# A two-layer hybrid decoder on one core: the whole program in one block, ordered against the library's timeline simulation

## The chip, the core and the metric

The kernel runs on one core of one Trainium2 chip. The metric is device time in microseconds (us) of one execution. Three executions of the kernel before took 1261.02, 1261.59 and 1265.77 us; the median is 1261.59 us.

## The reference

The input x is 512 tokens by 1024 channels, float32. Each of two layers does the following, all in float32:

```
h    = rmsnorm(x, attn_norm_w)
proj = h @ w_in                                  # z, xbc, dt, sc_*, q, k/v of three branches, gates
y_ssd = ssd_mixer(...)       # conv of width 4 + silu, chunked state-space scan (8 heads of 64, state 128), gated norm
y_sc  = sc_b * causal_dwconv(sc_c * sc_h)        # short convolution
y_nsa = nsa_mixer(...)       # 4 heads of 64: compressed, selected and window attention, weighted by gates
x = x + concat(y_ssd, y_sc, y_nsa) @ w_out
h = rmsnorm(x, ffn_norm_w)
gate, val = split(causal_dwconv(h @ w_up) + b)   # width 3, 2 x 2752 channels
x = x + (silu(gate) * val) @ w_down
```

and a last norm follows.

## The kernel before

Activations lie transposed, channels on the 128 partitions and the 512 tokens along a row. Every large product is made of three matmuls per 128x128 weight block (`mul3`, L188 to L190): weights and activations are each split into a rounded part and the rest (the weights by ACT L165 and then DVE or POOL L166), and the three significant cross products are accumulated in PSUM. One output tile of the input projection is 8 blocks, so 24 matmuls. In what follows these matmuls are called filler, since they can be placed wherever the rest leaves room.

A layer has three stretches. The first is the start: the norm's sums (ACT L224 squares, DVE L228 and L234 add, PE L236), their reciprocal root spread back over the partitions (DVE L201, POOL L202, PE L205, ACT L244), a group of narrow products (L450, L451) and the first projection tiles; rope (DVE L266 to L268), a split of keys (L282, L308) and the key compression (PE L468) follow. The second is attention: 32 head scores (PE L597 and L600, DVE L602 adds the mask and takes the row extreme, ACT L604 is the exponential, DVE L606 to L608 and DVE or POOL L610 scale it), each transposed by PE (L618), split by ACT L622 and DVE L625, and multiplied with the values (PE L637, tile `pv`, of which there is one). Between these pieces stand the projection's filler, the evacuation of its tiles (DVE L359) with the width-4 convolution (DVE L363, L365), and the small chain on time steps (`ssd_dt`, DVE L662 to L677). The third is the scan (L704 to L822) with its own norm, then the output projection. The gated MLP comes last, 65 tiles of up and down products, pure filler with its own evacuations.

The program is written in an order in which the pieces of attention and scan alternate with pieces of the projection, by weights in a table (`PLAN`). That text isn't yet the order on the engines. The library's tile layer takes the instructions as written and orders each engine's queue with a list scheduler that asks a simulation which instruction is ready and when; some instructions are kept in the order of the text (`pinned`). Each engine then runs its own queue strictly in order, and waits on semaphores where an operand comes from another engine. Line 1157 opens this scope:

```
with _tile.TileContext(nc) as tc:
    trunk(tc, ins, out)
```

Of the kernel before, what the change touches and what calls it, by code (L numbers as in the profile page):

```python
# [63 lines left out]
def trunk(ctx: ExitStack, tc: tile.TileContext, ins, out):  # L64
    nc = tc.nc
    V, A, G, TE = nc.vector, nc.scalar, nc.gpsimd, nc.tensor

    per = ctx.enter_context(tc.tile_pool(name="per", bufs=1))
    pw = ctx.enter_context(tc.tile_pool(name="pw", bufs=3))
    ph = ctx.enter_context(tc.tile_pool(name="ph", bufs=1))  # L70
# [1091 lines left out]
```

## Time and profile before

| | before |
|---|---|
| median of three executions | 1261.59 us |
| profiled execution | 1265.31 us, its span 1263.5 us |
| PE busy | 1208.4 us, 96% |
| DVE busy | 879.8 us, 70% |
| ACT, POOL busy | 580.8 and 221.8 us |
| mean granted clock of PE | 0.981 |

The profiled execution is 3.7 us, 0.3%, above the median, and 1.8 us of it lie outside its span. The span has five parts by time: mixers of layer 0 (0 to 253 us), MLP of layer 0 (253 to 632), mixers of layer 1 (632 to 885), MLP of layer 1 (885 to 1233), and the last norm with the output (1233 to 1263.5). A share of busy time over the whole span hides these parts, so the rows below take each by itself.

### The profile page before, as it was taken

Reading aid. Unit: us, or ns where it says so; the run is one execution under the profiler, and the core shown is the slowest. Engines: PE = TensorE matmul, PEld = TensorE weight load, DVE = VectorE, ACT = ScalarE, POOL = GpSimd, SP = SyncE. Lnnn points to the kernel's source line nnn. Section 1 sums busy time; section 2 is a strip of 40 time slices with the busy share of each in tenths; the row PEclk is TensorE's granted clock in tenths of the full one; section 3 lists DMA queues with packets and bytes.
Section 4 is the critical chain, followed back from the end, with each engine's and each line's share of the span. In section 5 each row is a group of like instructions: output and inputs, shape, how many; then the busy total and the mean of one; then the engine's idle time right before and its main releaser. Section 6 shows DMA issues by size and latency. Waiting matters only on the chain. (4 is left out here: it accounts for less than half of the span.)

```text
span 1263.5 us, 15487 instructions
## 1 busy us (share of the span) xinstructions
PE 1208.4 (96%) x5843; PEld 999.2 (79%) x5843; DVE 879.8 (70%) x1408; ACT 580.8 (46%) x909; POOL 221.8 (18%) x199
## 2 busy tenths in 40 slices
PE   8889899999999999999999888999999999999997
PEld 7667678788888888888877666778888888888897
DVE  6899979567776247776468998794587743677763
ACT  6655554354443124444347455434444422444553
POOL 3442337500000000000043332563000000000001
PEclk9989999999999999999999899999999999999999
DMA  7321123233223332332223211322233323333352
GB/s 259 113 67 51 51 84 101 67 100 98 88 98 100 100 99 90 95 117 87 84 84 100 67 51 51 103 98 83 84 100 101 100 88 96 100 100 100 122 165 99
DMA packets 37051, 121.33 MB, mean 96 GB/s; under 512 B 4144, under 2 KB 6512, under 8 KB 36976
## 3 DMA queue, kind: packets, MB, share of 16 engines
q1 hardware_dynamic: 36832, 120.33, 30.0%
q8 instruction: 46, 0.75, 0.3%
q14 instruction: 29, 0.24, 0.1%
q10 hardware_dynamic: 144, 0.00, 0.0%
HBM read 118.19 MB, written 2.13 MB: 95 GB/s over the span
## 5 line engine op out<-in xcount | busy, mean ns | idle before, releaser
L188 PE MATMUL mm<-h,hl 128*128 128x512 f32 x1040 | 413.6, 398 | 0.8 <-DVE s L359 0.8
L189 PE MATMUL mm<-h,hl 128*128 128x512 f32 x1040 | 410.3, 395 | 0.0
L190 PE MATMUL mm<-h,hl 128*128 128x512 f32 x1040 | 409.7, 394 | 0.0
L165 ACT ACTIVATE hl<-raw 128x1024 fp32r<-128x1024 f32 (+1 forms) x211 | 220.8, 1047 | 236.9 <-PE mm L190 129.5
L166 DVE TENSOR_TENSOR hl<-raw,hl 128x1024 fp32r<-128x1024 f32 (+1 forms) x167 | 203.4, 1219 | 110.3 <-ACT hl L165 108.1
L188 PEld LDWEIGHTS mm<-h,hl 128*128 128x128 f32 x1040 | 197.8, 190 | 42.0 <-issue 1.8
L190 PEld LDWEIGHTS mm<-h,hl 128*128 128x128 f32 x1040 | 197.4, 190 | 41.2 <-issue 0.2
L189 PEld LDWEIGHTS mm<-h,hl 128*128 128x128 f32 x1040 | 197.7, 190 | 39.6 <-issue 0.5
L202 POOL TENSOR_TENSOR m<-m,mhalf 128x1 f32<-128x1 f32 (+2 forms) x14 | 9.9, 709 | 773.7 <-DVE m L201 773.7
L166 POOL TENSOR_TENSOR hl<-raw,hl 128x1024 fp32r<-128x1024 f32 x44 | 108.3, 2464 | 150.5 <-ACT hl L165 144.8
L928 DVE SCALAR_TENSOR_TENSOR s<-s,par 128x511 f32<-128x511 f32 (+1 forms) x172 | 128.3, 748 | 3.5 <-ACT s L926 0.6
L925 DVE TENSOR_TENSOR s<-mm,rstdB 128x512 f32<-128x512 f32 x86 | 59.1, 689 | 66.1 <-PE mm L190 66.1
L189 PE MATMUL mm<-s,hl 128*128 128x512 f32 (+1 forms) x240 | 86.6, 361 | 3.4 <-DVE s L248 3.4
L188 PE MATMUL mm<-s,hl 128*128 128x512 f32 (+1 forms) x240 | 86.5, 360 | 1.1 <-ACT s L247 1.1
L190 PE MATMUL mm<-s,hl 128*128 128x512 f32 (+1 forms) x240 | 86.4, 360 | 0.0
L247 ACT ACTIVATE s<-s 128x512 fp32r<-128x512 f32 (+1 forms) x62 | 33.0, 545 | 111.8 <-DVE s L943 108.0
L188 PE MATMUL aux<-s,hl 128*128 128x512 f32 (+1 forms) x232 | 82.1, 354 | 0.0
L190 PE MATMUL aux<-s,hl 128*128 128x512 f32 (+1 forms) x232 | 81.8, 353 | 0.0
L189 PE MATMUL aux<-s,hl 128*128 128x512 f32 (+1 forms) x232 | 81.8, 353 | 0.0
L926 ACT ACTIVATE s<-s,par 128x512 f32<-128x512 f32 x86 | 69.2, 807 | 8.8 <-DVE s L925 8.1
L248 DVE TENSOR_TENSOR s<-s 128x512 fp32r<-128x512 f32 (+1 forms) x62 | 45.3, 741 | 27.9 <-ACT s L247 27.9
L941 ACT ACTIVATE s<-s 128x512 f32<-128x512 f32 x40 | 25.3, 632 | 79.0 <-DVE s L928 79.0
(252 smaller groups left out, 1648.9 us busy)
## 6 DMA issues: line engine op xcount, KB each, us to landing
raw<-in_w_up SPq DMA_DIRECT2D x86, 512.0 KB, 3.5
raw<-in_w_dn SPq DMA_DIRECT2D x54, 512.0 KB, 3.5
raw<-in_w_in SPq DMA_DIRECT2D x44, 512.0 KB, 3.5
raw<-in_w_out SPq DMA_DIRECT2D x16, 512.0 KB, 3.6
raw<-in_w SPq DMA_DIRECT2D x8, 512.0 KB, 3.6
s<-dr SPq DMA_DIRECT2D x16, 256.0 KB, 4.3
x<-in_xT SPq DMA_DIRECT2D x8, 256.0 KB, 5.8
out<-s SPq DMA_DIRECT2D x8, 256.0 KB, 3.4
```

What stands on the lines that cost most here:

```text
L165: A.activation(t[:, 0, a:b], r[:, a:b], AF.Copy)
L166: eng.tensor_tensor(t[:, 1, a:b], r[:, a:b], t[:, 0, a:b].bitcast(F32), op=OP.subtract)
L188: TE.matmul(ps, wh, rhs_h, start=first, stop=False)
L189: TE.matmul(ps, wh, rhs_l, start=False, stop=False)
L190: TE.matmul(ps, wl, rhs_h, start=False, stop=last)
L202: G.tensor_tensor(dst, v, mhalf[:, :n], op=OP.pow)
L247: A.activation(dst_h, src, AF.Copy)
L248: V.tensor_tensor(dst_l, src, dst_h.bitcast(F32), op=OP.subtract)
L925: V.tensor_tensor(u, ps, rstdB, op=OP.mult)
L926: A.activation(acc, u, AF.Identity, scale=w[:, 2:3], bias=pr[:, C_FCB + i:C_FCB + i + 1])
L928: V.scalar_tensor_tensor(acc[:, j:], u[:, :T - j], w[:, 2 - j:3 - j], acc[:, j:], op0=OP.mult, op1=OP.add)
L941: A.activation(g, g, AF.Silu)
```

## The change

```
@@ -65,6 +65,7 @@
     nc = tc.nc
     V, A, G, TE = nc.vector, nc.scalar, nc.gpsimd, nc.tensor
 
+    ctx.enter_context(tc.block(schedule_with_timeline_sim=True))
     per = ctx.enter_context(tc.tile_pool(name="per", bufs=1))
     pw = ctx.enter_context(tc.tile_pool(name="pw", bufs=3))
     ph = ctx.enter_context(tc.tile_pool(name="ph", bufs=1))
```

The whole program now stands in one block, and the order of each queue in that block is made with another simulation of the library, which keeps a timeline of the engines. No instruction is added to the work and none leaves it; each stays on its engine, and tiles and buffers are the same. Every line after L67 has a number higher by one. What differs is the order within the queues, nearly all of it in the two mixers. Three places follow, before and now.

The first is ACT at the start of layer 0, from the group's bias (L335, now L336) on. `rstdB` is the norm's factor spread over the partitions, on which the rope tables on DVE wait. Before:

```order
L335 ACTIVATE btmp<-aux,m 128x148 x2
L259 ACTIVATE s<-mm 128x512
L165 ACTIVATE hl<-raw 128x1024
L261 ACTIVATE s<-s 32x512
L262 ACTIVATE s<-s 32x512
L335 ACTIVATE btmp<-aux,m 128x148 x2
L347 ACTIVATE s<-s 128x4x64 x2
L350 ACTIVATE gate<-bS 128x48
L244 ACTIVATE rstdB<-pv 128x512
```

Now:

```order
L336 ACTIVATE btmp<-aux,m 128x148 x2
L166 ACTIVATE hl<-raw 128x1024 x2
L260 ACTIVATE s<-mm 128x512
L245 ACTIVATE rstdB<-pv 128x512
L262 ACTIVATE s<-s 32x512
L263 ACTIVATE s<-s 32x512
L166 ACTIVATE hl<-raw 128x1024
L336 ACTIVATE btmp<-aux,m 128x148 x2
```

The factor has moved ahead of the two copies of rope and of the second pair of bias rows. On DVE the product Cr (L399, now L400) has moved with it, ahead of the second pair of L336. On PE the spread (L205) stands 101 matmuls into the program, and stood 119 into it; the key compression (L468) stands at 197 and stood at 188.

The second is PE in the middle of layer 0's attention, where its scores of 256 columns (`128x256`) begin. `mm<-h` is filler. Before:

```order
L637 MATMUL pv<-s 128x512 x2
L618 MATMUL aux<-cst,s 128x128 x4
L190 MATMUL mm<-h_81,hl 128x512
L188 MATMUL mm<-h_82,hl 128x512
L637 MATMUL pv<-s 128x512
L189 MATMUL mm<-h_82,hl 128x512
L190 MATMUL mm<-h_82,hl 128x512
L188 MATMUL mm<-h_83,hl 128x512
L637 MATMUL pv<-s 128x512
L597 MATMUL aux<-s 128x256
```

Now:

```order
L638 MATMUL pv<-s 128x512 x2
L619 MATMUL aux<-cst,s 128x128 x4
L638 MATMUL pv<-s 128x512 x2
L598 MATMUL aux<-s 128x256
L601 MATMUL aux<-s 128x256
L598 MATMUL aux<-s 128x256
L601 MATMUL aux<-s 128x256
L598 MATMUL aux<-s 128x256
L601 MATMUL aux<-s 128x256
L189 MATMUL mm<-h_80,hl 128x512
```

The filler between the pieces of attention is gone; the last row here is the first of 23 filler matmuls in one lump. In matmuls 230 to 800 of the program there are now 29 runs of filler and 11 of them have 17 matmuls or more, where 48 runs stood before with 3 such; in layer 1 it is 27 with 10, where it was 48 with 3.

The third is DVE at the head of attention. `m` of `128x32` is the chain on time steps, `s<-aux,s` (L625, now L626) is the rest of a transposed score, without which the value product on PE can't be finished. Before:

```order
L666 RECIPROCAL m<-m 128x32
L625 TENSOR_TENSOR s<-aux,s 128x512
L667 TENSOR_TENSOR m<-m 128x32
L359 TENSOR_TENSOR s<-mm,rstdB 128x512
L668 TENSOR_TENSOR m<-m 128x32
L669 TENSOR_SCALAR m<-m 128x32
L671 SCALAR_TENSOR_TENSOR m<-m 128x32 x3
L363 SCALAR_TENSOR_TENSOR s<-s,cwh 128x511
L671 SCALAR_TENSOR_TENSOR m<-m 128x32
L625 TENSOR_TENSOR s<-aux,s 128x512
```

Now:

```order
L667 RECIPROCAL m<-m 128x32
L609 TENSOR_TENSOR m<-m,gate 128x4
L668 TENSOR_TENSOR m<-m 128x32
L611 TENSOR_SCALAR s<-s,m 128x512 x2
L669 TENSOR_TENSOR m<-m 128x32
L670 TENSOR_SCALAR m<-m 128x32
L672 SCALAR_TENSOR_TENSOR m<-m 128x32 x6
L673 SCALAR_TENSOR_TENSOR m<-m 128x32
L675 SCALAR_TENSOR_TENSOR dtk<-m 128x32
L678 SCALAR_TENSOR_TENSOR aa<-dtk,m 128x32
L626 TENSOR_TENSOR s<-aux,s 128x512
L360 TENSOR_TENSOR s<-mm,rstdB 128x512
```

The first of the rests has moved behind the whole chain, and the evacuation of a projection tile (L359, now L360) with it.

Elsewhere: in the scan two chunks now interleave where one followed the other; five matmuls of the output projection are written ahead of the scan's last products; in the MLP of either layer the spread of its norm stands 13 matmuls later, with 11 filler matmuls instead of 24 between it and the first matmul of the third tile; in layer 1's start the spread stands 14 matmuls later, L468 13 later, and ACT does two weight copies and one evacuation ahead of two copies of rope.

## Rows read from the trace of the kernel before

**Rows 1.** From the page: engines' busy us (share); a group's busy us, mean ns.

```profile
PE 1208.4 (96%) x5843; PEld 999.2 (79%) x5843; DVE 879.8 (70%) x1408; ACT 580.8 (46%) x909; POOL 221.8 (18%) x199
...
L165 ACT ACTIVATE hl<-raw 128x1024 fp32r<-128x1024 f32 (+1 forms) x211 | 220.8, 1047 | 236.9 <-PE mm L190 129.5
```

**Rows 2.** Five stretches: stretch, length, busy us (instructions) by engine, clock, DMA share, GB/s.

```profile
0.00:253.00 253.00, 228.37 (x1119) 182.88 (x1120) 205.54 (x404) 135.15 (x259) 110.17 (x98) 0.95 0.30 99
253.00:632.00 379.00, 378.86 (x1681) 313.47 (x1680) 237.54 (x298) 155.03 (x194) 1.41 (x2) 1.00 0.31 96
632.00:885.00 253.00, 231.44 (x1162) 186.17 (x1162) 200.80 (x401) 132.08 (x253) 103.56 (x91) 0.97 0.25 80
885.00:1233.00 348.00, 347.95 (x1708) 295.33 (x1707) 224.64 (x288) 148.99 (x189) 3.86 (x5) 1.00 0.34 106
1233.00:1263.50 30.50, 21.73 (x180) 21.32 (x178) 11.23 (x22) 9.58 (x18) 2.79 (x4) 0.90 0.28 94
```

**Rows 3.** The same view, attention and scan of either layer.

```profile
60.00:160.00 100.00, 88.44 (x417) 69.29 (x417) 92.67 (x196) 53.68 (x118) 35.06 (x24) 0.93 0.20 63
160.00:253.00 93.00, 88.61 (x468) 71.36 (x467) 68.80 (x150) 39.94 (x77) 50.81 (x51) 0.98 0.27 86
690.00:790.00 100.00, 86.28 (x423) 67.22 (x422) 90.19 (x190) 52.75 (x117) 32.63 (x25) 0.95 0.18 54
790.00:885.00 95.00, 90.84 (x471) 73.91 (x470) 69.76 (x137) 40.91 (x68) 49.29 (x46) 0.98 0.29 95
```

**Rows 4.** Waits of PE, 0 to 260 us: total, times, longest.

```profile
PE pv L637 <- DVE s L625: 6.3, 6, 2.1
PE aux L468 <- DVE s L308: 4.2, 1, 4.2
...
PE mm L189 <- DVE s L248: 1.7, 1, 1.7
```

**Rows 5.** The same wait in layer 1, 620 to 860 us.

```profile
PE aux L468 <- DVE s L308: 3.1, 1, 3.1
```

**Rows 6.** Waits of DVE, 20 to 60 us.

```profile
DVE s L336 <- ACT btmp L335: 4.5, 2, 3.0
```

**Rows 7.** Timeline of PE: start, us, instruction, idle before and its releaser.

```profile
48.29 3.00 PE L468 MATMUL aux<-hl,s 128*64 128x256 f32 x16 [4.17 <-DVE s L308]
51.09 0.63 PE L190 MATMUL mm<-h,hl 128*128 128x512 f32 x1
51.52 0.63 PE L188 MATMUL mm<-h,hl 128*128 128x512 f32 x1
...
59.06 0.50 PE L597 MATMUL aux<-s 128*128 128x512 f32 x1 [1.22 <-DVE s L325]
```

**Rows 8.** Timeline of ACT at the first norm.

```profile
30.87 0.58 ACT L244 ACTIVATE rstdB<-pv 128x512 f32<-128x512 f32 x1
```

**Rows 9.** Timeline of DVE at the first norm.

```profile
31.48 0.69 DVE L399 TENSOR_TENSOR Cr<-rot,rstdB 128x512 f32<-128x512 f32 x1
...
47.07 1.17 DVE L308 TENSOR_TENSOR s<-s 128x256 fp32r<-128x256 f32 x2
```

**Rows 10.** Timeline of DVE, 76 to 86 us.

```profile
76.59 0.63 DVE L625 TENSOR_TENSOR s<-aux,s 128x512 fp32r<-128x512 f32 x1
...
82.94 2.34 DVE L671 SCALAR_TENSOR_TENSOR m<-m 128x32 f32<-128x32 f32 x1
...
85.80 0.17 DVE L671 SCALAR_TENSOR_TENSOR m<-m 128x32 f32<-128x32 f32 x1
```

**Rows 11.** Timeline of PE at the second value product.

```profile
85.94 0.50 PE L637 MATMUL pv<-s 128*128 128x512 f32 x1 [1.57 <-DVE s L625]
...
87.22 0.63 PE L190 MATMUL mm<-h,hl 128*128 128x512 f32 x1
```

**Rows 12.** Timeline at the start of layer 0's gated MLP, PE and DVE.

```profile
288.64 0.60 PE L205 MATMUL pv<-cst,m 128*128 128x128 f32 x4
...
291.12 1.28 DVE L925 TENSOR_TENSOR s<-mm,rstdB 128x512 f32<-128x512 f32 x2
```

More of the change, by code (lines that the diff above doesn't have):

```diff
@@ L66, in trunk @@
     V, A, G, TE = nc.vector, nc.scalar, nc.gpsimd, nc.tensor
+    ctx.enter_context(tc.block(schedule_with_timeline_sim=True))
     per = ctx.enter_context(tc.tile_pool(name="per", bufs=1))
```

## The prediction

> **What bounds the kernel now.** The busy times by engine come first [rows 1]: PE works 1208.4 of 1263.5 us, so an order can win back no more than the 55.1 us in which PE idles, and what its clock loses. The windows say where these lie [rows 2]. In the two MLP stretches PE is busy 378.86 of 379 us and 347.95 of 348 us at a clock of 1.00; nothing is to be had there, and a matmul costs 379/1681 = 0.225 us. The mixers hold 253 - 228.37 = 24.6 us of idle PE in layer 0 and 253 - 231.44 = 21.6 us in layer 1; the last norm holds 8.8 us, and its order hardly differs. So the change is decided in the mixers.
>
> Within them I read the finer windows [rows 3]. In layer 0's attention (60 to 160 us) DVE is busy 92.67% and PE 88.44%, in layer 1's 90.19% and 86.28%: DVE sets the pace, PE follows 12 to 14 us short of full. From there to the output projection it turns round: PE has 88.61 of 93 us, and 90.84 of 95, DVE 73 to 74%. A new order can only shorten attention by what DVE idles there, 7.3 us and 9.8 us, and the stretch after it by what PE idles, 4.4 and 4.2 us, unless work moves from one stretch into another. The waits of PE name the places: in layer 0 the products with the values wait 6.3 us for DVE's rests, the key compression waits once per layer, 4.2 and 3.1 us, and the output projection waits 1.7 us for a normed tile [rows 4, 5].
>
> **The change part by part.** All sums are against the profiled execution, 1265.3 us, which lies 3.7 us above the median; the difference is then taken from the median.
>
> Start of layer 0. Before, ACT makes `rstdB` at 30.87 us, behind a pair of bias rows and the values' split, and DVE, which had waited 4.5 us in two waits for such rows, starts its rope tables at 31.48 [rows 6, 8, 9]. Now the factor stands ahead of the second bias pair and of two rope copies, and the spread on PE comes 18 matmuls, 18 x 0.225 = 4.1 us, sooner. Cr can start some 3 to 3.5 us sooner, but of what DVE did between its waits about 2 us come after it now; the split of keys (L308, 47.07 us [rows 9]) comes 1.5 to 2 us sooner. The key compression waits 4.17 us for it at 48.29 [rows 7]. It now has nine more filler matmuls ahead, 2.0 us: so the wait falls to 4.17 - 1.8 - 2.0 = about 0.4 us, and PE is 3.8 us of work further on. Behind the old wait the next matmuls come 0.425 us apart (51.09, 51.52) and the clock of the stretch is 0.95 [rows 2, 7]; that loss goes as well. The first score stood at 59.06, behind another 1.22 us of waiting for DVE [rows 7]. Between DVE's 1.5 us and PE's gain of 3.8 plus 1 for the clock, I take 3 us: bounds -1.5 and -4.8.
>
> Attention of layer 0. The chain on time steps now stands whole ahead of the first rest. By [rows 10] its pieces take 0.17 us by themselves and 2.34 us where they run beside POOL; twelve instructions are 2 us if all run alone, and about 8 us if three of them are stretched. The first value product waits so much longer, and with it stand behind it on PE 4 + 4 + 4 small matmuls and then 17 filler ones. DVE does the same work in either order, so this costs PE, which has 11.6 us to spare in the stretch, and not DVE. I take nothing. After it DVE gets its scores in bursts, and waits for PE through a lump of about 20 filler matmuls, 4.5 us, if its own queue runs dry meanwhile. It doesn't as long as it has evacuations, convolutions and rests for the length of a lump; at 92.67% busy it is behind more often than ahead. Bounds: all of DVE's idle time gone, -7.3 us, and 8 more long lumps at 2 us each (45% of a lump), +16. On POOL weight splits now stand ahead of two scalings of scores; the longest delay of that kind on the rows is 2.3 us [rows 10], inside these bounds. The weight loads on SP move by a few places, with DMA at 0.30 of its time in the stretch [rows 2]: nothing. I take 0, which is nearer to the row of its busy share than either end.
>
> Scan and end of layer 0. PE is the later engine, with 4.4 us of idle time [rows 3]. The interleaved chunks and the five matmuls written ahead give it work in the 1.7 us wait for the normed tile [rows 4]. Bounds 0 and -4.4; I take -2.
>
> Start of layer 1. ACT's three instructions ahead of the rope copies are two weight copies of 1.05 us [rows 1] and an evacuation, over 2.1 us, of which I take DVE to feel some 1.3 us. L468 comes 13 matmuls, 2.9 us, later, so that its wait of 3.1 us falls to about 1.5 [rows 5]. PE gains 1.6 us, DVE loses 1.3: I take +1, since DVE sets the pace next; bounds -1.6 and +2.5.
>
> Attention and end of layer 1. As in layer 0: 0 (bounds -9.8 and 7 lumps x 2 = +14), and -2 (0 to -4.2).
>
> MLP. Before, the spread is issued at 288.64 and the evacuation that frees a bank for the third tile starts at 291.12 and has done its first tile by about 291.8 [rows 12]: 3.1 us of chain, covered by 24 matmuls and more, 5.4 us. Now 11 matmuls cover 2.5 us, so 0.6 us of wait appear, in each layer: +0.5 each; bounds 0 and +0.8. The other matmuls of the MLP run at 100% either way: 0. The last norm: 0.
>
> Sum: -3 + 0 - 2 + 1 + 0 - 2 + 1 = -5 us. 1265.3 becomes 1260.3 in a profile; 1261.6 becomes 1256.6.
>
> A rule of the Trainium skill speaks against the new order. First the row: after the 1.57 us wait at 85.94 and the 4.17 us one at 48.29 PE ran matmuls of 0.63 us [rows 7, 11], and layer 0's mixers have a clock of 0.95, which is 5% of 253 = 12.7 us of matmul time lost, layer 1's 0.97, 7.6 us [rows 2]. "TensorE: Matmul & The Clock Gate" (Part 1, on the clock gate) says that an array which falls idle between bursts is set back to 1.2 GHz and that a loop should be arranged to avoid such pauses. By that rule bursts of attention without filler are just what lowers the clock, and the sum would be up to 12.7 us higher. The trace agrees that pauses are followed by slow matmuls; how many more pauses there will be it doesn't show, so the rule gets a rival of its own.
>
> **The rivals.** A: the forecast, -5 us, own range -11 to +2: 1251 to 1264.
>
> B: much faster. For it speaks that the filler which PE ran while attention was ready is now out of its way; DVE would get its scores the moment they can be made and idle no more. Then its 7.3 and 9.8 us go, most of them: -5 - 13 = -18, 1243.6 us. Against it: 92.67% is already high, and DVE's waits there are for many engines.
>
> C: slower, by lumps. 15 more long lumps stand in front of scores and value products; if DVE empties its queue 1 us before the end of each, that is +15: 1261.6 - 5 + 15 = 1271.6 us. It decides from the point at which DVE has under 3.5 us of work when a lump starts. For it: the three head scores ahead of a lump give DVE three short instructions, the rest has to come from evacuations and rests. Against it: DVE's idle time is only 7.3 us now, and its work is the same.
>
> D: slower, by clock. If the pauses in attention cost layer 0 as much again as it loses now, 12.7 us, and layer 1 the same, and half lies under DVE's pace, it is +12.7: 1261.6 - 5 + 12.7 = 1269.3 us.
>
> E: no difference. DVE's pace absorbs the start, what PE gains is waited away in the first value product (8 us there), and the end stays: 1261.6. That the flag changes nothing is excluded by the order itself.
>
> **How the numbers follow.** A 0.44, B 0.18, C 0.23, D 0.07, E 0.08. About 0.5%, 6.3 us, can be told from no change. Of A some 0.20 lies below 1255.3 and 0.24 within; B is all faster; C and D give 0.26 slower and 0.04 within; E is within. So faster 0.38, same 0.36, slower 0.26. The range leaves out the lower half of B and a third of C and D: 1244 to 1273. A alone is 1251 to 1264.
>
> **What would show it.** In the profile of the changed kernel: `rstdB` before 28.5 us and a wait of L469 under 1.5 us, with the first score by 56 us, would bear out the start. DVE at 92% or more through attention, and no wait for PE over 2 us on it, would bear out the zero; waits of DVE for L598/L601 or L619 of 1 us and more behind each lump would be C, a clock under 0.93 in the mixers D. The wait for the first value product should be 3 to 8 us. Layer 0's MLP should begin 4 to 6 us sooner, with a wait of about 0.6 us at its third tile. A start of the MLP no sooner than 253 us, or PE under 86% in attention, would make the forecast wrong.

## The result, and the profile after

The changed kernel takes 1301.68 us (median of four, 1300.46 to 1303.75) beside 1262.68 for the one before on the same chip: a ratio of 1.032, 95% interval 1.030 to 1.034. It is 39 us slower, where 5 us faster was forecast and the range ended at 1273.

The profiled execution took 1303.75 us, span 1302.0. From its page, the busy times that answer to [rows 1]:

```profile
span 1302.0 us, 15519 instructions
...
PE 1227.5 (94%) x5843; PEld 1017.3 (78%) x5843; DVE 879.4 (68%) x1408; ACT 582.0 (45%) x909; POOL 229.0 (18%) x199
```

PE is busy 19.1 us longer with the same 5843 matmuls, which run at half clock more often, and idles 74.5 us where it idled 55.1, 19.4 us more: by this count the 38.5 us that the span gained are half slower matmuls and half idle time. Next the windows, cut at the first score, the last value product and the end of the scan of each layer. First before (stretch, length, busy us of PE, PEld, DVE, ACT, POOL, clock, DMA share, GB/s):

```profile
59.00:177.00 118.00, 106.22 (x501) 82.53 (x501) 106.35 (x233) 64.20 (x144) 36.95 (x28) 0.94 0.21 68
177.00:247.00 70.00, 65.78 (x359) 53.69 (x359) 54.38 (x111) 28.72 (x48) 46.13 (x45) 0.98 0.26 83
674.00:795.00 121.00, 106.74 (x515) 82.63 (x513) 105.20 (x231) 68.37 (x148) 39.17 (x29) 0.96 0.23 68
795.00:865.00 70.00, 65.84 (x359) 53.59 (x359) 54.05 (x110) 28.71 (x48) 45.80 (x45) 0.98 0.25 83
```

Then the same stretches of the changed kernel, with its start and its first MLP:

```profile
0.00:60.00 60.00, 54.21 (x243) 45.38 (x244) 45.41 (x60) 40.92 (x67) 23.89 (x24) 0.91 0.54 179
60.00:199.00 139.00, 120.91 (x553) 96.33 (x552) 106.04 (x231) 66.89 (x146) 44.08 (x32) 0.90 0.19 61
199.00:269.00 70.00, 58.88 (x305) 46.52 (x305) 52.88 (x112) 26.14 (x46) 42.25 (x43) 0.93 0.24 76
269.00:653.00 384.00, 384.00 (x1710) 318.55 (x1709) 239.15 (x300) 157.38 (x196) 4.38 (x2) 1.00 0.31 96
697.00:839.00 142.00, 122.12 (x551) 97.64 (x551) 108.36 (x232) 70.58 (x152) 44.84 (x31) 0.89 0.18 56
839.00:905.00 66.00, 57.48 (x302) 45.17 (x302) 50.08 (x110) 25.92 (x45) 41.95 (x43) 0.92 0.26 80
```

Attention takes 139 us instead of 118 in layer 0, and 142 instead of 121 in layer 1: by these cuts all of the loss. Some 9 and 7 us of it, by an estimate, are filler that has moved in: counted in the order of PE's queue, 41 matmuls in layer 0 and 29 in layer 1, at 0.225 us each. DVE has the same work there (106.04 and 106.35 us), so that its share falls from 90% to 76%. PE's clock falls from 0.94 to 0.90. The scan is no longer than before (70 us, and 66 in layer 1), but it should have been shorter: in layer 0 PE runs 305 instead of 359 instructions in it, 51 filler matmuls (11.5 us) having moved ahead, 41 of them into attention and 10 in front of the first score. PE idles 11.1 us there instead of 4.2. The MLP is full at 384.00 of 384 us, as before.

The waits in layer 0's attention, of PE and then of DVE (total, times, longest):

```profile
PE pv L638 <- DVE s L626: 8.9, 3, 4.7
PE aux L619 <- POOL s L611: 3.3, 1, 3.3
```

```profile
DVE s L626 <- ACT s L623: 7.3, 4, 5.6
DVE s L603 <- PE aux L601: 6.2, 4, 2.1
```

Waits of DVE for scores (L603 on L601) are new; before has none in attention. They are the smaller part of its new waiting: DVE's waits on ACT add up to 24.2 us in this view, and to 11.6 in the same view of before. The longest of them, 5.6 us, leads back to PE: the last transposes of a head stand behind 21 filler matmuls, which started at 171.94, and ACT and then DVE wait for them. PE, ACT and DVE:

```profile
178.99 0.40 PE L191 MATMUL mm<-h,hl 128*128 128x512 f32 x1
179.22 1.04 PE L619 MATMUL aux<-cst,s 128*128 128x128 f32 x8
```

```profile
179.92 1.09 ACT L623 ACTIVATE s<-aux 128x512 fp32r<-128x512 f32 x2 [6.22 <-PE aux L619]
```

```profile
180.55 1.29 DVE L626 TENSOR_TENSOR s<-aux,s 128x512 fp32r<-128x512 f32 x2 [5.60 <-ACT s L623]
```

### The profile page after: what moved, and what is told of

The parts are those of the page before. It is cut to its first block, busy times and chain, and to the rows that moved or that the text cites. A ratio compares the mean times of both kernels' runs of the same rounds, so it can differ in the third digit from the quotient of the medians.

```text
span 1302.0 us, 15519 instructions
## 1 busy us (share of the span) xinstructions
PE 1227.5 (94%) x5843; PEld 1017.3 (78%) x5843; DVE 879.4 (68%) x1408; ACT 582.0 (45%) x909; POOL 229.0 (18%) x199
## 5 line engine op out<-in xcount | busy, mean ns | idle before, releaser
L203 POOL TENSOR_TENSOR m<-m,mhalf 128x1 f32<-128x1 f32 (+2 forms) x14 | 12.9, 918 | 775.4 <-DVE m L202 775.4
L190 PE MATMUL aux<-s,hl 128*128 128x512 f32 (+1 forms) x232 | 81.8, 353 | 0.0
L191 PE MATMUL aux<-s,hl 128*128 128x512 f32 (+1 forms) x232 | 81.8, 352 | 0.0
L638 PE MATMUL pv<-s 128*128 128x512 f32 x80 | 32.4, 449 | 25.2 <-DVE s L626 17.1
L249 DVE TENSOR_TENSOR s<-s 128x512 fp32r<-128x512 f32 (+1 forms) x62 | 35.7, 586 | 28.7 <-ACT s L248 28.7
```

What stands on the lines that cost most here:

```text
L190: TE.matmul(ps, wh, rhs_l, start=False, stop=False)
L191: TE.matmul(ps, wl, rhs_h, start=False, stop=last)
L203: G.tensor_tensor(dst, v, mhalf[:, :n], op=OP.pow)
L249: V.tensor_tensor(dst_l, src, dst_h.bitcast(F32), op=OP.subtract)
L638: o_ = TE.matmul(acc, v, p_, start=first and i == 0, stop=(b == 2))
```

## The experiments

The library can be told that an instruction follows another on its engine. With that the queue of any engine can be held to a given order, while the order of the others is either held as well or left to the scheduler. The edit is one function, called at the end of the program with a table of places:

```
+def hold(tc, eng, kinds, code):
+    rows = [i for i in tc.nc.cur_bb.bb.instructions if i.engine == eng and type(i).__name__ in kinds]
+    order = ...                                  # the table: places of rows, in the order wanted
+    for a, b in zip(order, order[1:]):
+        tc.add_manual_dep(rows[b], rows[a].name, ...NoSync..., reason="order")
```

The theories at the outset: 1, PE's order costs (rival C among its forms); 2, the queues of DVE and POOL cost, since they hold PE up at the head of attention.

**e1**, the block alone. Edit: `ctx.enter_context(tc.block())`, without the flag.

> The one block, with the default order in it: no flag. The queues of all engines hold the same order as before. If the block itself (its entry and end) costs, this shows it: up to +40 us. If the order alone decides, this stays within 0.3% of before, 1259 to 1266 us.

1260.21 us, ratio 0.9995 (0.998 to 1.001). The block costs nothing that these runs can show.

**e2 to e4**, one engine's order each.

```
e2: after   + hold(PE, order of after), hold(DVE, ACT, POOL, order of before)
e3: after   + hold(PE, order of before)
e4: after   + hold(POOL, order of before), hold(PE, DVE, ACT, order of after)
```

> The order of before on DVE, ACT and POOL, the new order on PE alone. Theory 1, PE's order is the cause (scores and value products in bursts, filler in lumps of about 20): 1285 to 1305 us, DVE under 85% busy in attention. Theory 2, the cause lies in the queues of DVE and POOL (the time-step chain ahead of the first rest, the weight splits ahead of the scalings), which hold PE up: here 1258 to 1270 us.

> The block with the timeline order, but PE held to its order of before; DVE, ACT and POOL are ordered around that by the timeline. Theory 1: 1258 to 1270 us. Theory 2: 1280 us or more, since the chain and the splits still stand in front.

> The new order on PE, DVE and ACT, POOL alone in its order of before, so that the scalings of scores are ahead of the weight splits again. In the changed kernel the first transposed score waits 3.31 us for such a scaling. Theory 1: 1297 to 1303 us, the wait goes and comes back elsewhere. Theory 2: 6 us or more gained (3.3 us in each of two layers), 1288 to 1296 us.

e2 1308.62 us (1.038, 1.036 to 1.039), e3 1257.49 (0.998, 0.996 to 0.999), e4 1321.03 (1.048, 1.046 to 1.049). PE's order by itself makes the whole loss, and with PE's order of before the flag is even worth some 3 us. Theory 2 fell with these two. Giving POOL alone its old order costs another 20 us, presumably because the other queues were made to fit the new one; no run shows that by itself.

**e5, e6, e11, e12**, parts of PE's order, all other engines held to before's.

```
e5:  hold(PE, order of after between first score and last value product, else before)
e6:  hold(PE, the complement of e5)
e11: hold(PE, order of after in the scan only)
e12: hold(PE, order of after from the norm's sums to the first score only)
```

> As e2, but PE takes the new order only within attention (first score to last value product of either layer); start, scan, output projection and MLP on PE, and all of DVE, ACT and POOL, stand as before. If the bursts and lumps of attention are the cause: 1290 to 1308 us, most of e2's 47. If what moved around attention is (start, scan, end): under 1275 us.

> The complement of e5: PE has the new order everywhere but in attention, the rest as before. If attention is the cause: 1255 to 1272 us. If the start, the scan and the end are: 1285 us or more. If the parts add, e5 and e6 together lose about the 47 us of e2.

> PE in the new order only in the scan, from the last value product to the first 30 matmuls of the output projection; all else as before. In e6 the scan took 12 us longer in each layer. If its interleaved chunks are the reason: 1280 to 1290 us. If it came from elsewhere: 1259 to 1267 us.

> PE in the new order only from the norm's sums to the first score, in either layer; all else as before. The prediction took 3 us off layer 0 here and put 1 us on layer 1, in company with the new orders of ACT and DVE. With those of before: 1260 to 1268 us if the start is worth little either way; 1270 or more if PE's later key compression holds the first scores up.

e5 1292.95 (1.024), e6 1290.78 (1.023), e11 1287.46 (1.018), e12 1268.94 (1.005, 1.004 to 1.007). Attention and scan each lose when PE's order alone is changed, and the start loses some 7 us; the sum of e5 and e6 is more than e2's 47 us, so the parts don't add. In e11 DVE stands in the scan before products that PE now makes later (its waits from 177 to 260 us):

```profile
DVE cbm L736 <- PE aux L732: 6.8, 1, 6.8
DVE s L822 <- PE aux L205: 5.6, 2, 2.9
DVE s L783 <- PE aux L775: 5.4, 1, 5.4
```

That left open what is due to queues that don't fit each other, so two were repeated with the others ordered by the timeline.

**e17, e18**, as e5 and e6, with the block and its flag.

> As e5 (PE in the new order in attention only), but DVE, ACT and POOL ordered by the timeline around it, as in the changed kernel. If the lumps cost whatever the other queues do: 1283 to 1296 us. If the other queues' fitting order makes up for them: 1257 to 1272 us.

> As e6 (PE in the new order everywhere but in attention), with the timeline's order on the others. If the scan's loss in e6 and e11 came from PE standing against DVE, ACT and POOL queues of another order: 1255 to 1270 us. If the interleaved chunks cost by themselves: 1280 us or more.

e17 1293.52 (1.026, 1.023 to 1.028), e18 1269.67 (1.007, 1.004 to 1.009). Against e3, which treats the other queues in the same way, the new order in attention costs 35 us by the ratios and the new order elsewhere 11; the changed kernel costs 43. Fitting queues help the scan (75.1 and 76.9 us in e18 from the last value product to the last DVE instruction of the scan's norm, 82.2 and 84.3 in e11), attention not at all. The traces of e18 and e3, whose profiled runs lie 16 us apart, also tell where the 11 us come from. The scans of e3 take 66.8 us in both layers, 8 and 10 us less than those of e18. Layer 1's attention is 3 us longer in e18, and the first score of layer 0 comes sooner, at 58.76 us instead of 60.94. So it is the scan's new order that loses, and the start gains about 2 us.

**e7, e8**, filler spread.

```
e7: after + hold(PE, order of after, each lump in attention cut into pieces of 2 to 5 behind its attention pieces)
e8: after + hold(PE, order of the text)
```

> The changed kernel with the same sequence of scores, transposes and value products on PE, but in attention each lump of filler is spread in pieces of 2 to 5 over the attention pieces that follow it; DVE, ACT and POOL ordered by the timeline around that. If the lumps are the cause: 1258 to 1275 us. If it is the sequence of the attention pieces (bursts): 1290 us or more.

> The block with the timeline order, but PE kept in the order of the program text, where filler stands in pieces of 3 to 9 between attention pieces; the rest by the timeline. If the cause is that the timeline order gathers filler into lumps: 1255 to 1275 us. If any order that puts attention pieces together in groups of 4 to 8 loses, as the text does too: 1285 us or more.

e7 1297.32 (1.029), e8 1302.10 (1.032). Both missed what the lump theory expected: small pieces alone don't bring the time back. In e7 no run of filler in attention is longer than 8 matmuls in layer 0 and 13 in layer 1, and still DVE waits for scores in the two attentions more than in the changed kernel (17.0 us; its row, 14.6, stands further down):

```profile
DVE s L603 <- PE aux L601: 17.0, 22, 2.9
```

What e7 keeps is much of the lead: counted in PE's order, an attention piece has 14 (layer 0) and 19 (layer 1) more filler matmuls ahead of it on the mean than before, at most 48; in the changed kernel it is 24 and 28, at most 64. Whether so long a lead costs by itself was not tried and stays open. In e8 it is the other way: no run is longer than 9, and a piece has 21 and 18 fewer filler matmuls ahead of it than before. So it has neither lumps nor such a lead; PE's order is another in all stretches there, and why it loses stays open. PE idles 22.1 and 16.6 us in layer 0's attention of e7 and e8, against 11.7 before. The next two runs tell the sequence of attention pieces from the place of the filler.

**e9, e10**, filler and sequence, other engines held to before's order.

```
e9:  hold(PE, attention pieces in before's sequence, ahead of each as much filler as in after)
e10: hold(PE, attention pieces in after's sequence, ahead of each as much filler as in before)
```

> Before's sequence of scores, transposes and value products on PE, but in attention the filler stands in the lumps of the changed kernel (17 to 24 in a run, the same filler as before in all); DVE, ACT and POOL as before. If the lumps are the cause: like e5, 1283 to 1296 us, with DVE waiting for scores. If the sequence (bursts) is: 1258 to 1270 us.

> The complement of e9: the changed kernel's sequence of attention pieces, with as much filler ahead of each piece as before; DVE, ACT and POOL as before. If the sequence is the cause: 1283 to 1296 us. If the lumps are: 1258 to 1270 us. If each needs the other, both stay under 1275 us while e5 has 1293.

e9 1294.54 (1.025, 1.022 to 1.027), e10 1264.79 (1.001, 1.000 to 1.003). The sequence is worth next to nothing; where the filler stands makes the 31 us. That place is lumps and lead together: in e9 an attention piece has 21 and 25 more filler matmuls ahead of it on the mean than before, at most 49. One lump of e9, PE and then DVE (start, us, instruction, idle before and its releaser):

```profile
134.31 0.80 PE L637 MATMUL pv<-s 128*128 128x512 f32 x1 [2.69 <-DVE s L625]
...
135.97 0.41 PE L600 MATMUL aux<-s 128*128 128x256 f32 x1
136.19 0.63 PE L188 MATMUL mm<-h,hl 128*128 128x512 f32 x1
136.62 0.63 PE L189 MATMUL mm<-h,hl 128*128 128x512 f32 x1
...
138.90 0.39 PE L189 MATMUL mm<-h,hl 128*128 128x512 f32 x1
...
142.99 0.28 PE L597 MATMUL aux<-s 128*128 128x256 f32 x1
143.10 0.28 PE L600 MATMUL aux<-s 128*128 128x256 f32 x1
```

```profile
139.44 0.09 DVE L602 DVE_READ_ACCUMULATOR2_ANT m<- 128x1 f32 x1
139.60 0.69 DVE L365 SCALAR_TENSOR_TENSOR s<-s 128x512 f32<-128x512 f32 x1
143.42 0.42 DVE L602 CUSTOM_DVE_ANT_0 s<-aux,cst 128x256 f32<-128x256 f32 x1 [3.13 <-PE aux L600]
```

Three of four head scores are made by 136.2; then PE runs 24 filler matmuls, and one value product among the last of them, until 142.99. DVE masks the three, does a rest and its convolution (L363, L365) and has nothing more from 140.3 on: it waits 3.13 us for the fourth score. The lump is 6.8 us long and not 4.5, because it has 25 matmuls and not 20, and because behind PE's wait of 2.69 us its first matmuls, up to 138.3, come 0.43 us apart and the later ones 0.23.

**e13 to e15**, how long a lump and how far ahead, all else as before.

```
e13: hold(PE, filler behind the key compression in lumps of 20, at the place of each lump's first matmul)
e14: the same with lumps of 10
e15: small pieces as before, 10 more filler matmuls ahead of every attention piece
```

> Before's order on all engines, but in attention (behind the key compression) filler on PE stands in lumps of 20, each drawn together at the place of its first matmul: on the mean a piece has 10 more filler matmuls ahead of it, at most 19, and never the 45 of e9. If lumps are the cause: about e9, 1283 to 1298 us. If the lead is: like e15, and under 1275 us.

> As e13 with lumps of 10, mean lead 5 matmuls. If a lump costs by what it exceeds of the work that DVE has in hand: under half of e13's loss, 1264 to 1276 us. If every regrouping loses the same: as e13.

> Before's order on all engines and its small pieces of filler, but from the key compression on ten more filler matmuls, 2.3 us, stand ahead of every attention piece, drawn from the end of attention. If the lead is the cause: 1270 us or more. If lumps are: 1260 to 1267 us, a delay of about 2 us per layer at the most.

e13 1279.13 (1.015, 1.013 to 1.017), e14 1260.07 (1.000, 0.999 to 1.001), e15 1259.47 (0.998, 0.996 to 1.000). Twenty in a run cost 18.5 us, ten nothing, and a lead of ten nothing. e13 fell between its two expectations: lumps cost without a long lead, but not all of e9's 31 us. Between first score and last value product e13 has 11 and 12 runs of 17 matmuls or more in the two layers, before has 3 and 3: 17 more, so that one costs about 1.1 us, an estimate. e9 has only 8 and 8 and loses more. So lumps of this length explain a part. The plain difference in the rest is e9's longer lead, but no run has that alone. Nor does length decide alone: before's own three runs in each layer, of 19 to 26, stand where DVE waits for no score. This fits a lump that costs by what it outlasts of DVE's work in hand, as in the one shown. The waits of DVE for scores in both attentions say the same. In e9, then e13, then the changed kernel (in before, e10, e14 and e15 there is no such row):

```profile
DVE s L602 <- PE aux L600: 12.0, 6, 3.6
```

```profile
DVE s L602 <- PE aux L600: 8.1, 4, 2.8
```

```profile
DVE s L603 <- PE aux L601: 14.6, 11, 3.4
```

**e16**, the best of both.

```
e16: before + hold(PE, order of before), hold(DVE, ACT, POOL, e3's order in attention and scan, else before)
```

> Before's order on PE, and on all engines in the starts and the MLP; DVE, ACT and POOL have e3's timeline order in attention and scan. e3 was 4 us faster than before with a start that was 2 us slower in layer 0 and 3 us in layer 1. If the gain lies in attention and scan: 1250 to 1255 us. If the order of the other queues is worth nothing by itself: 1259 to 1264 us.

1251.72 us, 0.993 (0.991 to 0.995): faster than both kernels. From its page and windows:

```profile
span 1247.6 us, 15497 instructions
```

```profile
177.00:247.00 70.00, 67.65 (x376) 55.58 (x375) 52.83 (x111) 28.27 (x46) 50.45 (x46) 1.00 0.29 91
```

PE is busy 67.65 of these 70 us, before 65.78, at a clock of 1.00 instead of 0.98. By the timeline layer 0's scan takes 66.9 us instead of 70.6, and layer 1's attention 115.1 instead of 120.5. So in attention and scan the timeline's order is better here than the default on DVE, ACT and POOL, and worse on PE.

## Why the prediction was wrong, by its steps

**The step that failed** is "I take 0" for attention, on the ground that DVE at 92.67% busy [rows 3] is behind more often than ahead and so doesn't run dry in a lump. It does: its share falls to 76%. PE's new order in attention costs 35 us (e17 against e3), and it is the place of the filler that costs, 31 us in e9, not the sequence of the pieces (e10). That share came with the small pieces: before, DVE never waited for a score. What should have been compared is one lump with the work that DVE can do without PE, which in the lump shown is 4.1 us (136.2 to 140.3) against 6.8.

The bound that stood beside the zero, 2 us for each of 15 long lumps, 16 + 14 = 30 us, is close to e9's 31, but by luck: e13 pays about 1.1 us a lump, and e9 has its loss with fewer lumps and a longer lead. Rival C, with a chance of 0.23, had the place and the mechanism of the lumps, and with 1 us a lump nearly the price that e13 gives; it doesn't cover the rest of the loss. Its sign, a wait for scores of 1 us and more behind each lump, came only in part: three such waits (1.8, 1.9 and 2.1 us) for ten long lumps in layer 0's attention.

**The filler's lead** was not priced: 41 more filler matmuls stand in layer 0's attention, 29 in layer 1's. In the scan, which before had 4.4 us of idle PE [rows 3], they are missed. I forecast 2 us of gain in each; layer 0's scan kept its length and layer 1's became 4 us shorter, with 11.5 us less filler in either. By e18 the order outside attention costs 11 us, in place of the -5 that start, scan and MLP were to bring.

**Start of layer 0**: `rstdB` did come sooner, at 27.17 us instead of 30.87 [rows 8], but not the first score, at 60.27 instead of 59.06 [rows 7]. On ACT, PE and DVE:

```profile
27.17 0.59 ACT L245 ACTIVATE rstdB<-pv 128x512 f32<-128x512 f32 x1
```

```profile
46.06 0.50 PE L191 MATMUL mm<-h,hl 128*128 128x512 f32 x1 [2.19 <-DVE hl L167]
...
51.89 1.98 PE L469 MATMUL aux<-hl,s 128*64 128x256 f32 x16
...
60.27 0.39 PE L598 MATMUL aux<-s 128*128 128x512 f32 x1
```

```profile
49.24 1.10 DVE L309 TENSOR_TENSOR s<-s 128x256 fp32r<-128x256 f32 x3
```

The key compression has no wait left, as forecast; PE now waits 2.19 us for a weight split that DVE does later, and the split of keys came 2.2 us later than at 47.07 [rows 9], not 2 us sooner. I had moved one instruction and not the queue behind it. -3 became +1.2; as ten more filler matmuls (2.3 us) are done by then, the start gained about 1 us in work.

**Start of layer 1**: the wait of 3.1 us for the key compression [rows 5] is gone, but from the group's first product to the first score it takes 46.7 us (650.71 to 697.37) instead of 44.1, with 22 more filler matmuls in it: +2.6 where I took +1.

**Head of attention**: the wait for the chain on time steps came as forecast (3 to 8 us), 4.69:

```profile
73.81 0.33 PE L619 MATMUL aux<-cst,s 128*128 128x128 f32 x1 [3.31 <-POOL s L611]
...
84.16 0.79 PE L638 MATMUL pv<-s 128*128 128x512 f32 x1 [4.69 <-DVE s L626]
...
88.91 0.63 PE L190 MATMUL mm<-h,hl 128*128 128x512 f32 x1
```

```profile
77.24 5.51 DVE L672 SCALAR_TENSOR_TENSOR m<-m 128x32 f32<-128x32 f32 x6
...
83.42 0.68 DVE L626 TENSOR_TENSOR s<-aux,s 128x512 fp32r<-128x512 f32 x1
```

I said it costs PE and not DVE. PE's idle time is not free here: the matmuls behind it run at 0.63 us, and all that stands behind it in PE's queue comes later.

**Clock**: rival D's rule, from the Trainium skill ("TensorE: Matmul & The Clock Gate", Part 1), was that pauses lower the clock. The trace agrees: 0.90 in attention against 0.94, and 0.43 us between matmuls behind the 2.69 us wait above. 0.90 also meets D's sign, a clock under 0.93. By PE's busy time, half of what the span gained is slower matmuls. The runs don't separate what the pauses would cost at full clock, so C and D aren't told apart in full; the lower clock lengthens each lump that follows a wait.

**MLP**: the 0.6 us wait at the third tile didn't appear; PE is busy 384.00 of 384 us. That term should have been 0.

That the change does what it says, that the MLP and the last norm keep their length, and that it is decided in the mixers, was right. What a long lead costs by itself, and why e8 loses, stays open.

## What to carry to other kernels

Where two engines feed each other, compare the longest run of independent work on the one with what the other has in hand without it; a busy share says little on that, since it depends on how finely the work was interleaved. Filler in runs of 10 was free here and in runs of 20 cost 18.5 us; lumps with a long lead cost 31. Cutting lumps up without taking back their lead (e7) brought back little. An order made by another simulation can be taken engine by engine: hold the one queue whose old order is better, and let the new one order the rest.

## What the runs showed of the hardware

Small DVE instructions beside weight splits on POOL: six of 128x32 took 5.51 us from 77.24 on (one takes 0.17 alone [rows 10]). POOL was at work from 77.14 to 81.8, and the first two of the six lasted until 79.55 and 81.85, its two subtractions until 79.50 and 81.80; the other four then took 0.19 us each. POOL, then DVE:

```profile
77.14 4.66 POOL L167 TENSOR_TENSOR hl<-raw,hl 128x1024 fp32r<-128x1024 f32 x2
```

```profile
77.24 2.31 DVE L672 SCALAR_TENSOR_TENSOR m<-m 128x32 f32<-128x32 f32 x1
79.59 2.26 DVE L672 SCALAR_TENSOR_TENSOR m<-m 128x32 f32<-128x32 f32 x1
```

The Trainium skill ("SBUF — State Buffer", Summary: rules for kernel authors) says that a DVE instruction with two SBUF inputs and a POOL instruction that reads SBUF keep the second of them blocked until the first has finished; these rows agree, and here it lay on the path to the first value product.
